# A third of a layer's modulation vectors kept early, two thirds computed one layer later

## The chip, the cores and the metric

The kernel runs on one core of one Trainium2 chip. A core has a matrix engine (TensorE, PE in the rows), a vector engine (VectorE, DVE), a scalar engine with table functions (ScalarE, ACT), a general engine (GpSimd, POOL) and SyncE (SP), which only issues transfers here. ACT and POOL issue transfers too. The metric is the device time of one execution in microseconds (us); the kernel before and the changed one are compared by the median of their timed runs.

## The reference

The program is two layers over 512 latent and 256 context rows of width 1024. What matters here, for each layer l:

```
mod      = silu([c, c_ctx]) @ w_ada[l] + b_ada[l]      # two rows of 6 x 1024
sh1, sc1, ga1, sh2, sc2, ga2 = split(mod, 6)
h        = rmsnorm(x, g_mix[l]) * (1 + sc1) + sh1
parts    = split(h @ w_in[l])                          # 1024 x 2560
y        = [neighbourhood attention, RG-LRU scan, differential attention](parts)
x        = x + ga1 * (y @ w_out[l])
h2       = rmsnorm(x, g_ffn[l]) * (1 + sc2) + sh2
x        = x + ga2 * mixture_of_experts(h2)            # 32 experts, 2 of 8 in one of 4 groups
```

The modulation vectors of a layer depend on c, c_ctx and w_ada[l] alone, not on x. The first third (sh1, sc1) is needed before that layer's projections. The other two thirds (ga1, sh2, then sc2, ga2) are needed only behind its w_out product. w_ada[l] is 24 MB of weights for two rows.

## The kernel before, in words

A layer opens with the norm of x, then forms h as a high and a low half (hh, hl) and runs its input projections. The projections go in chunks of 256 columns of w_in, named by their first column: 768 and 1024 (RG-LRU input), 0, 256, 512 (queries, keys, values of the neighbourhood attention), 2304, 1792, 2048 (values, queries, keys of the differential attention), 1280 and 1536 (gate). A chunk is one 1 MB transfer on SP's queue (line 392); ACT casts it to its high half (line 434) and DVE subtracts for the low half (line 435). A product is 24 matmuls at line 491: high by high, high by low, low by high. A product of context rows or values has 256 columns, one of latent rows 512.

The products stand in a list, `fill`, and `run_fill` (lines 525 to 536) works through it twice in a layer: the first list runs beside the RG-LRU scan, the second beside the neighbourhood attention. Behind every product it fetches the next chunk and calls `step()`. The scan runs in parts (m = 0 to 3, two directions d): for each, gate matmuls on PE (line 753) need an input cast by ACT (xh) and subtracted by DVE (xl, line 435), ACT takes two sigmoids (tt, ii, line 754) and further functions (lines 755, 756, 769), and DVE multiplies and scans (lines 758 and 775 to 793).

`step()` is one modulation step. `ada_steps` (lines 353 to 382) makes a layer's vectors in three groups of 2048 columns, eight steps each. A step is one 1 MB transfer of w_ada on SP's queue (line 360) and four matmuls (line 362) with 32 stationary columns (scp, of which two are real) into the four quarters of one accumulator, acc; the trace records each of the four as two passes. Before a group's first step two small transfers on ACT's queue fetch its bias into adab (line 357). Behind its eighth step DVE adds bias and accumulator into adas (line 367) and ACT's queue carries the two stores to DRAM (line 370); group 0 alone is also transposed and put in columns (lines 374 to 379). Before the change `step()` works only in layer 0. Of the 48 steps eight run at the very start (layer 0, group 0) and 40 stand between layer 0's products: 16 for its own groups 1 and 2, 24 for layer 1.

All w_ada and w_in transfers, and the halves of the chunks, take turns in one ring of six 1 MB buffers (`wtile`, pool `wt`): a transfer waits until the buffer it takes over has been read. An engine works through its instructions in the order of the program, and a scheduler that builds the program has set that order; pools hold the temporary buffers. Later in a layer the same ring carries w_out, and the experts' weights stream through it and through others behind it, by SP.

Of the kernel before, what the change touches and what calls it, by code (L numbers as in the profile page):

```python
# [8 lines left out]
F32 = mybir.dt.float32  # L9
# [3 lines left out]
AF = mybir.ActivationFunctionType  # L13
# [237 lines left out]
def program(tc, a, out, dbg=None):  # L251
# [23 lines left out]
    V, S, G, T = [Chained(e_) for e_ in (nc.vector, nc.scalar, nc.gpsimd, nc.tensor)]  # L275
# [33 lines left out]
    def pacc():  # L309
        return ps.tile([128, 512], F32, name="acc", bufs=1)  # L310
# [24 lines left out]
    cc = con.tile([128, 16], F32, name="cc")  # L335
# [4 lines left out]
    adab = [None, None, None]  # L340
# [9 lines left out]
        else:  # L350
            eng.tensor_copy(o, i)  # L351

    def ada_steps(l):
        for g in range(3):
            acc = pacc()
            for v in range(2):
                S.dma_start(adab[0][v:128:32], a["b_ada"][l].rearrange("(g j f) -> g j f", g=3, j=4)[g])
# [25 lines left out]
    adag = [None, None]  # L383
# [38 lines left out]
    cur = [0]  # L422

    def step(n=1):
        if cur[0] == 0:
            for _ in range(n):
                for g in adag:
                    if next(g, 0) != 0:
                        break

    ct = lambda c_, x_, y_: x_ if c_ else y_

# [19 lines left out]
    for l in range(2):  # L452
# [11 lines left out]
        yp, vp, hp_, xrp, xnp = nxt  # L464
# [3 lines left out]
        if l == 0:  # L468
            trf = hp_.tile([128, 128], F32, name="trf")
            S.dma_start(trf, a["cst"][:, C_TRI:C_MSK])  # L470
            V.tensor_copy(tri, trf)
            scp = hp_.tile([128, 8, 32], F32, name="scp")
            V.memset(scp, 0.0)
            S.activation(scp[:, :, 0:2], cc.rearrange("p (k v) -> p k v", v=2), AF.Silu)
            adab[:] = [hp_.tile([128, 512], F32, name="adab"), hp_, scp]
            G.memset(adab[0], 0.0)
            adag[0] = ada_steps(0)
            adag[1] = ada_steps(1)
        chunks = {}

        def getw(c0):
# [48 lines left out]
        def run_fill(each, then=()):  # L530
            for i_, (c0, f) in enumerate(fill):
                each(i_)
                f()
                for c1 in ([c_ for c_, _ in fill] + list(then))[i_ + 1:i_ + 1 + AHEAD]:
                    getw(c1)
                step()
# [23 lines left out]
        groups = ((4, 2), (0, 2), (2, 2))  # L560
# [948 lines left out]
        def place(s):  # L1509
            return s if s < nm else nm + (s - nm) // 2 if s < nr else s - np_  # L1510

        def column(s):
            return idn[:, place(s), :]
# [459 lines left out]
        for n_ in range(NE + 1):  # L1973
            f = None
            if n_ < NE:
# [4 lines left out]
                else:  # L1980
                    g = Group(column(s), slots[:, place(s):place(s) + 1] if SCT[l] and n_ < NE - 2 else None)
# [104 lines left out]
        g = es[-1].g  # L2086
# [76 lines left out]
```

## Time and profile before

| | |
|---|---|
| timed, median of 3 runs | 2044.59 us |
| lowest, highest | 2043.42, 2047.09 us |
| the profiled execution, its own time | 2047.19 us |
| its span (first to last instruction) | 2045.6 us |
| mean granted TensorE clock | 0.909 |
| busy: PE, DVE, ACT, POOL | 1692.9, 901.0, 575.3, 407.1 us |
| bytes moved | 579.20 MB |

The profile is of one execution, whose time is 2.6 us above the median of the timed runs. Busy shares are averages over stages that differ much: in layer 0 the first list runs from about 60 to 210 us and the second to 341 us; the experts of layer 0 follow to about 1090 us; layer 1's first list runs from about 1125 to 1285 us, its second to 1365 us, and its experts' weights stream from about 1420 us to the end. A granted clock of 1.00 is 2.4 GHz, 0.50 is 1.2 GHz.

### The profile page before, as it was taken

What the parts mean: (1) busy time and instruction counts of PE and PEld (TensorE: products, weight loads), DVE (VectorE), ACT (ScalarE), POOL (GpSimd) and SP (SyncE); (2) the same over time, 40 slices, a digit from 0 to 9 for tenths busy, and PEclk for the clock granted to TensorE, in tenths of its full rate; (3) what the DMA queues carried; (4) which work ended last, traced back from release to release, by engine and by line L of the source; (5) the groups of instructions that cost most, each with busy time, mean ns of one, the idle gap of its engine ahead of it and who ended that gap; (6) DMA issues with size and microseconds to landing.
All of it is one profiled execution on the core that took longest, in us unless ns stands there. A gap on an engine that the chain in (4) does not pass through costs nothing. (4 is left out here: it accounts for less than half of the span.)

```text
span 2045.6 us, 24880 instructions
## 1 busy us (share of the span) xinstructions
PE 1692.9 (83%) x9306; PEld 975.2 (48%) x9306; DVE 901.0 (44%) x1506; ACT 575.3 (28%) x1033; POOL 407.1 (20%) x394
## 2 busy tenths in 40 slices
PE   4998998899697888889895987887959988879773
PEld 3766666676333333333333977566733333333221
DVE  3876443785622212212227698548662122121225
ACT  3563343662111101111113475346411010010011
POOL 1344000443311011001003145104321110010001
PEclk8999999898698998999896989898969989999886
DMA  8537967606799989989986113346469999999994
GB/s 299 203 131 285 322 225 185 165 37 252 275 409 348 407 344 368 417 325 410 401 342 261 58 51 103 125 111 207 188 228 400 404 414 409 410 413 416 416 392 167
DMA packets 153709, 579.20 MB, mean 283 GB/s; under 512 B 18734, under 2 KB 54958, under 8 KB 114672
## 3 DMA queue, kind: packets, MB, share of 16 engines
q1 hardware_dynamic: 142240, 553.35, 71.5%
q0 software_dynamic: 9328, 20.87, 2.9%
q10 hardware_dynamic: 2016, 3.34, 0.5%
q8 instruction: 75, 1.23, 0.2%
q14 instruction: 50, 0.41, 0.1%
HBM read 544.74 MB, written 42.05 MB: 287 GB/s over the span
## 5 line engine op out<-in xcount | busy, mean ns | idle before, releaser
L491 PE MATMUL mm<-hh,w 128*128 128x256 f32 (+1 forms) x960 | 191.5, 343 | 6.6 <-ACT w L434 4.7
L1643 PE MATMUL pss<-w,xT 128*64 128x512 f32 x368 | 170.7, 611 | 7.3 <-DMA w<-in_w_dram 7.3
L1642 PE MATMUL pss<-w,xT 128*64 128x512 f32 x368 | 175.3, 619 | 0.0
L1638 PE MATMUL pss<-w,xT 128*32 128x512 f32 x880 | 140.4, 686 | 37.2 <-DMA w<-in_w_dram 37.2
L491 PEld LDWEIGHTS mm<-hh,w 128*128 128x128 f32 x960 | 150.1, 193 | 37.7 <-issue 9.8
L1826 POOL DMA_INDIRECT xg<-h2d,idx_t x64 | 61.4, 959 | 515.7 <-PE mm L1628 476.8
L1648 PE MATMUL pss<-w,xT 128*128 128x512 f32 x352 | 156.0, 597 | 0.0
L1658 ACT COPY hs<-pss 128x512 f32<-128x512 f32 x53 | 30.9, 582 | 375.6 <-PE pss L1638 221.9
L1517 POOL DMA_INDIRECT yd<-yl,slots x47 | 44.3, 942 | 383.1 <-DVE yl L1562 204.3
L1700 PE MATMUL pss<-w,hT 128*64 128x512 f32 x184 | 102.0, 698 | 9.2 <-DVE hT L1678 8.9
L1648 PEld LDWEIGHTS pss<-w,xT 128*128 128x128 f32 x352 | 65.3, 190 | 89.1 <-issue 83.3
L1678 DVE TENSOR_TENSOR hT<-hT,mm 128x128 f32<-128x128 f32 (+1 forms) x53 | 18.3, 345 | 196.0 <-ACT hT L1677 195.9
L1701 PE MATMUL pss<-w,hT 128*64 128x512 f32 x184 | 102.0, 698 | 0.0
L1558 DVE SCALAR_TENSOR_TENSOR yl<-g,wsl,yl 64x1024 f32<-64x1024 f32 (+2 forms) x32 | 40.8, 1276 | 129.9 <-ACT yl L1553 129.6
L1638 PEld LDWEIGHTS pss<-w,xT 128*32 128x32 f32 x880 | 32.0, 122 | 137.7 <-issue 74.5
L1553 ACT ACTIVATE yl<-g,wsl 64x1024 f32<-64x1024 f32 (+2 forms) x32 | 36.6, 1147 | 211.2 <-DMA yd<-yl,slots 178.6
L1706 PE MATMUL pss<-w,hT 128*128 128x512 f32 x176 | 91.0, 664 | 3.1 <-issue 3.1
L491 PE MATMUL mm<-hl,w 128*128 128x256 f32 (+1 forms) x480 | 93.2, 336 | 0.1
L1562 DVE TENSOR_TENSOR yl<-pss,yl 64x512 f32<-64x512 f32 (+1 forms) x44 | 29.6, 687 | 138.7 <-PE pss L1701 76.0
L351 DVE COPY xT<-mm 128x512 f32<-128x512 f32 (+1 forms) x64 | 36.2, 566 | 101.2 <-PE mm L1628 100.5
L491 PEld LDWEIGHTS mm<-hl,w 128*128 128x128 f32 x480 | 75.4, 190 | 11.1 <-issue 0.8
L1643 PEld LDWEIGHTS pss<-w,xT 128*64 128x64 f32 x368 | 48.8, 140 | 60.3 <-issue 48.2
(377 smaller groups left out, 3263.4 us busy)
## 6 DMA issues: line engine op xcount, KB each, us to landing
w<-in_w_dram SPq DMA_DIRECT2D x382, 1024.0 KB
w<-in_w_ada_dram SPq DMA_DIRECT2D x48, 1024.0 KB
w<-in_w_in_dram SPq DMA_DIRECT2D x20, 1024.0 KB
yd<-bm SPq DMA_DIRECT2D x20, 512.0 KB
w<-yd SPq DMA_DIRECT2D x10, 1024.0 KB
ks<-st SPq DMA_DIRECT2D x16, 384.0 KB
w<-in_w_out_dram SPq DMA_DIRECT2D x5, 1024.0 KB
h2d<-hp SPq DMA_DIRECT2D x10, 512.0 KB
```

The source lines that it names most:

```text
L491: i_ = T.matmul(o, x_(k), y_(k), start=(n == 0), stop=(n == 23))
L1517: G.indirect_dma_start(out=yd[l][0:2 * nrow, :], out_offset=bass.IndirectOffsetOnAxis(ap=idxt, axis=0), in_=rows, in_offset=None, bounds_c ...
L1553: S.activation(self.u[r], g2[r, 1], AF.Copy, scale=b_)
L1558: (V if eng[1] == "V" else G).scalar_tensor_tensor(self.u[r], g2[r, 0], a_, self.u[r], op0=ALU.mult, op1=ALU.add)
L1638: T.matmul(ph[32 * g:32 * g + 32, 0:512], xT[:, k + g // 2, 0:32], w(k + g // 2), start=(k == 0), stop=(k == 6))
L1642: T.matmul(ph[0:64, 0:512], xT[:, k, 0:64], w1(k), start=(k == 0), stop=(k == 7))
L1643: T.matmul(ph[64:128, 0:512], xT[:, k, 0:64], w3(k), start=(k == 0), stop=(k == 7))
L1648: T.matmul(ph[:, o:o + 512], xT[:, k, :], w(k), start=(k == 0), stop=(k == 7))
L1700: T.matmul(py[0:64, :], hT[:, k, 0:64], w2(k, 0), start=(k == 0), stop=(k == 3))
L1701: T.matmul(py[64:128, :], hT[:, k, 0:64], w2(k, 1), start=(k == 0), stop=(k == 3))
L1706: T.matmul(self.p[:, 512 * hf:512 * hf + 512], hT[:, k, :], w2(k, hf), start=(k == 0), stop=(k == 3))
L1826: G.indirect_dma_start(out=o[0:n_, :], out_offset=None, in_=h2d[l][0:nrow, :], in_offset=bass.IndirectOffsetOnAxis(ap=idxt, axis=0), bound ...
```

## The change

`ada_steps` takes a list of groups. Layer 0 now makes only group 0 of layer 1's vectors; layer 1 sets up the stationary tile scp and the bias tile adab anew and makes groups 1 and 2 itself. `step()` works in both layers. So layer 0's lists carry 24 steps in place of 40, and layer 1's first list carries 16.

```diff
--- before.py
+++ after.py
@@ -350,8 +350,8 @@
         else:
             eng.tensor_copy(o, i)
 
-    def ada_steps(l):
-        for g in range(3):
+    def ada_steps(l, groups=(0, 1, 2)):
+        for g in groups:
             acc = pacc()
             for v in range(2):
                 S.dma_start(adab[0][v:128:32], a["b_ada"][l].rearrange("(g j f) -> g j f", g=3, j=4)[g])
@@ -422,11 +422,10 @@
     cur = [0]
 
     def step(n=1):
-        if cur[0] == 0:
-            for _ in range(n):
-                for g in adag:
-                    if next(g, 0) != 0:
-                        break
+        for _ in range(n):
+            for g in adag:
+                if next(g, 0) != 0:
+                    break
 
     ct = lambda c_, x_, y_: x_ if c_ else y_
 
@@ -475,7 +474,14 @@
             adab[:] = [hp_.tile([128, 512], F32, name="adab"), hp_, scp]
             G.memset(adab[0], 0.0)
             adag[0] = ada_steps(0)
-            adag[1] = ada_steps(1)
+            adag[1] = ada_steps(1, (0,))
+        else:
+            scp = hp_.tile([128, 8, 32], F32, name="scp")
+            V.memset(scp, 0.0)
+            S.activation(scp[:, :, 0:2], cc.rearrange("p (k v) -> p k v", v=2), AF.Silu)
+            adab[:] = [hp_.tile([128, 512], F32, name="adab"), hp_, scp]
+            G.memset(adab[0], 0.0)
+            adag[:] = [ada_steps(1, (1, 2))]
         chunks = {}
 
         def getw(c0):
```

In the order of instructions, on PE, near the end of layer 0's second list (hh, hl and w are a product's halves, qa, ka, pe, pT and po belong to the neighbourhood attention). Before:

```order
L491 MATMUL mm<-hh,w 128x256 x8
L491 MATMUL mm<-hl,w 128x256 x8
L491 MATMUL mm<-hh,w 128x256 x8
L362 MATMUL acc<-w,scp 32x512 x4
L899 MATMUL mm<-cst,pe 128x128 x4
L916 MATMUL po<-pT,vv 64x128 x4
L491 MATMUL mm<-hh,w 128x512 x8
L491 MATMUL mm<-hl,w 128x512 x8
L491 MATMUL mm<-hh,w 128x512 x8
L362 MATMUL acc<-w,scp 32x512 x4
L916 MATMUL po<-pT,vv 64x128 x4
```

In the changed kernel, the same place:

```order
L497 MATMUL mm<-hh,w 128x256 x8
L497 MATMUL mm<-hl,w 128x256 x8
L497 MATMUL mm<-hh,w 128x256 x8
L905 MATMUL mm<-cst,pe 128x128 x4
L922 MATMUL po<-pT,vv 64x128 x4
L497 MATMUL mm<-hh,w 128x512 x8
L497 MATMUL mm<-hl,w 128x512 x8
L497 MATMUL mm<-hh,w 128x512 x8
L922 MATMUL po<-pT,vv 64x128 x4
L497 MATMUL mm<-hh,w 128x256 x8
```

The step (the rows with acc) is gone from between the products; all that stands around it keeps its order. Sixteen such groups of four are gone from PE's order between the first list's last value products and the end of the second list.

On PE in layer 1's first list, from a key product (hh,w and hl,w, chunk 256) to the value products behind it (w,hh and w,hl, chunk 512; xh, xl, gh and gl are the operands of the gate matmuls). Before:

```order
L491 MATMUL mm<-hh,w 128x256 x8
L491 MATMUL mm<-hl,w 128x256 x8
L491 MATMUL mm<-hh,w 128x256 x8
L491 MATMUL mm<-w,hh 128x256 x16
L491 MATMUL mm<-w,hl 128x256 x8
L491 MATMUL mm<-w,hh 128x256 x16
L491 MATMUL mm<-w,hl 128x256 x8
L753 MATMUL mm<-xh,gh 128x512
L753 MATMUL mm<-xl,gh 128x512
L753 MATMUL mm<-xh,gl 128x512
L753 MATMUL mm<-xh,gh 128x256
L753 MATMUL mm<-xl,gh 128x256
```

In the changed kernel:

```order
L497 MATMUL mm<-hh,w 128x256 x8
L497 MATMUL mm<-hl,w 128x256 x8
L497 MATMUL mm<-hh,w 128x256 x8
L362 MATMUL acc<-w,scp 32x512 x4
L497 MATMUL mm<-w,hh 128x256 x16
L497 MATMUL mm<-w,hl 128x256 x8
L362 MATMUL acc<-w,scp 32x512 x4
L497 MATMUL mm<-w,hh 128x256 x16
L497 MATMUL mm<-w,hl 128x256 x8
L362 MATMUL acc<-w,scp 32x512 x4
L759 MATMUL mm<-xh,gh 128x512
L759 MATMUL mm<-xl,gh 128x512
```

A step now stands behind each of the first 16 products of the list, three of them in these rows, and the gate matmuls, whose result ACT takes up, stand behind the third.

On ACT in layer 1, at part m = 2 of the scan (v is a store of values, vv their copy). Before:

```order
L754 ACTIVATE tt<-mm,hbr 128x512
L754 ACTIVATE tt<-mm,hbr 128x256
L754 ACTIVATE ii<-mm,hbi 128x512
L754 ACTIVATE ii<-mm,hbi 128x256
L755 ACTIVATE ae<-tt,cfm 128x768
L821 DMA v_8074<-vv 64x256
L756 ACTIVATE tt<-tt,cf 128x768
L754 ACTIVATE tt<-mm,hbr 128x512
L822 DMA v_8074<-vv 64x256
L754 ACTIVATE tt<-mm,hbr 128x256
```

In the changed kernel:

```order
L760 ACTIVATE tt<-mm,hbr 128x512
L370 DMA ada_58<-adas 4x512 x2
L760 ACTIVATE tt<-mm,hbr 128x256
L760 ACTIVATE ii<-mm,hbi 128x512
L760 ACTIVATE ii<-mm,hbi 128x256
L761 ACTIVATE ae<-tt,cfm 128x768
L828 DMA v_7969<-vv 64x256
L762 ACTIVATE tt<-tt,cf 128x768
L357 DMA adab<-in_b_ada_dram 4x512 x2
L760 ACTIVATE tt<-mm,hbr 128x512
L760 ACTIVATE tt<-mm,hbr 128x256
L760 ACTIVATE ii<-mm,hbi 128x512
```

Group 1's two stores of adas stand between the halves of the first sigmoid of one direction, and group 2's two bias transfers ahead of the next direction's first sigmoid.

On ACT at the start of layer 1's second list (raw and rh belong to the RG-LRU state and rotary code, w is a chunk). Before:

```order
L918 COPY yT<-po 128x128
L434 CAST rh<-raw 128x512
L933 COPY raw<-mm 128x512
L434 CAST w<-w 128x2048
L434 CAST rh<-raw 128x512
```

In the changed kernel:

```order
L349 COPY pT<-mm 128x512
L433 CAST rh<-raw 128x512
L433 CAST w<-w 128x2048
L939 COPY raw<-mm 128x512
L924 COPY yT<-po 128x128
```

In both kernels the last cast of a chunk in the first list is the one ahead of this place. Of the casts here the one before is chunk 1280's and follows the copy raw; in the changed kernel it is chunk 2048's, which was cast in the first list before, and it stands between the cast rh and the copy raw.

## Rows read from the trace of the kernel before

**Rows 1.** The page: PE's busy time, share, instructions; the chain that ended last.
```profile
PE 1692.9 (83%) x9306; PEld 975.2 (48%) x9306; DVE 901.0 (44%) x1506; ACT 575.3 (28%) x1033; POOL 407.1 (20%) x394
...
DMA 13%; PE 7%; DVE 1%; ACT 0%; issue 0%; POOL 0%; POOLq 0%; SPq 0%; DVEq 0%; ACTq 0%
```

**Rows 2.** Stages of layer 0: PE, PEld, DVE, ACT, POOL busy (x), clock, DMA share, GB/s.
```profile
208.40:341.20 132.80, 132.12 (x892) 93.00 (x892) 58.26 (x131) 55.48 (x107) 5.85 (x5) 1.00 0.71 242
341.20:360.00 18.80, 10.42 (x41) 7.65 (x40) 8.10 (x12) 4.99 (x9) 3.03 (x2) 0.92 1.05 224
```

**Rows 3.** Line 362 in all: ns min/median/max, first, last; us and times it waited.
```profile
L362 PE MATMUL acc<-w,scp x384: 592/592/617, 23.6 to 332.0; 128*32 128x512 f32 x192
...
  DMA w<-in_w_ada_dram: 11.0, 8
```

**Rows 4.** PE in layer 0: start, us, line, operation, tiles, count, [idle before <-releaser].
```profile
318.96 1.07 PE L362 MATMUL acc<-w,scp 128*32 128x512 f32 x8
319.96 0.66 PE L899 MATMUL mm<-cst,pe 128*128 128x128 f32 x4
```

**Rows 5.** PE behind layer 0's second list, columns as in rows 4.
```profile
342.18 0.74 PE L1132 MATMUL pss<-w,yh 128*128 128x512 f32 x2 [0.93 <-ACT yh L434]
...
357.53 1.62 PE L267 MATMUL pss<-ks,qs 128*128 128x512 f32 x4 [4.94 <-DMA X<-in_x_dram]
```

**Rows 6.** Stages of layer 1's lists, columns as in rows 2.
```profile
1188.50:1285.00 96.50, 68.96 (x441) 62.65 (x441) 87.35 (x78) 55.48 (x74) 44.61 (x26) 0.88 0.29 95
1300.00:1365.00 65.00, 65.00 (x412) 50.16 (x412) 33.63 (x71) 28.98 (x56) 5.08 (x4) 0.98 0.25 82
```

**Rows 7.** PE in layer 1's lists, where it stood idle, columns as in rows 4.
```profile
1193.09 0.57 PE L753 MATMUL mm<-xl,gh 128*128 128x512 f32 x1 [4.56 <-DVE xl L435]
...
1218.77 0.79 PE L753 MATMUL mm<-xl,gh 128*128 128x512 f32 x1 [5.52 <-DVE xl L435]
...
1248.47 0.80 PE L753 MATMUL mm<-xh,gh 128*128 128x512 f32 x1 [7.82 <-ACT tt L754]
...
1284.72 2.08 PE L935 MATMUL mm<-raw,cst 128*128 128x512 f32 x2 [9.51 <-ACT raw L933]
...
1298.75 1.67 PE L935 MATMUL mm<-raw,cst 128*128 128x512 f32 x2 [2.23 <-ACT raw L933]
...
1309.86 1.13 PE L935 MATMUL mm<-raw,cst 128*128 128x512 f32 x2
```

**Rows 8.** ACT in layer 1's first and second lists, columns as in rows 4.
```profile
1220.03 1.11 ACT L754 ACTIVATE tt<-mm,hbr 128x512 f32<-128x512 f32 x2 [2.56 <-PE mm L753]
...
1228.25 0.69 ACT L754 ACTIVATE tt<-mm,hbr 128x512 f32<-128x512 f32 x1 [3.21 <-PE mm L753]
...
1235.20 1.58 ACT L769 ACTIVATE sq<-tt 128x768 f32<-128x768 f32 x2
...
1298.59 1.90 ACT L434 CAST w<-w 128x2048 fp32r<-128x2048 f32 x1
```

**Rows 9.** DVE in layer 1's first list, columns as in rows 4.
```profile
1224.78 1.31 DVE L788 TENSOR_TENSOR_SCAN sq<-tt,ii 128x256 f32<-128x256 f32 x1
...
1236.16 5.15 DVE L775 SCALAR_TENSOR_TENSOR tt<-tt,ae 128x768 f32<-128x768 f32 x2 [0.82 <-ACT sq L769]
...
1279.77 2.27 DVE L435 TENSOR_TENSOR w<-w 128x2048 fp32r<-128x2048 f32 x1
```

**Rows 10.** ACT in layer 0's first list, at a store of adas, columns as in rows 4.
```profile
113.98 1.06 ACTq L370 DMA_DIRECT2D ada<-adas  x2
115.14 1.06 ACT L754 ACTIVATE tt<-mm,hbr 128x512 f32<-128x512 f32 x2 [3.83 <-issue]
```

**Rows 11.** The set-up of scp: engine, line, operation, count, ns, start.
```profile
L473 DVE MEMSET scp<- x1: 272/272/272, 1.2 to 1.2; 128x256 f32 x1
L474 ACT ACTIVATE scp<-cc x1: 217/217/217, 5.9 to 5.9; 128x16 f32<-128x16 f32 x1
```

**Rows 12.** The add of bias and accumulator, columns as in rows 11.
```profile
L367 DVE TENSOR_TENSOR adas<-acc,adab x6: 676/692/693, 33.4 to 332.7; 128x512 f32<-128x512 f32 x6
```

## The prediction

> **What bounds the kernel now.** I read the page first. PE is busy 83% of the span, and the chain that ended last is transfers of expert weights and PE [rows 1], so the change can only tell where it touches PE's own time or a chain that PE waits for. Next I read the time by stretches. In layer 0, from 208.4 to 341.2 us, PE is busy 132.12 of 132.80 us at a granted clock of 1.00, DVE 58.26 and ACT 55.48 [rows 2]: a stage bounded by PE alone. All sixteen steps that leave layer 0 stand in it or within a few us of it. In layer 1 the picture is the reverse. From 1188.5 to 1285 PE is busy 68.96 of 96.50 us and DVE 87.35 [rows 6]: here the chain of the RG-LRU parts through DVE and ACT is the bound, and PE stands idle four times, 4.56, 5.52, 7.82 and 9.51 us, once more 2.23 [rows 7]. From 1300 to 1365 PE is full again [rows 6]. So the work moves from a stretch where PE is the bound to one where it is not, and the question is what the second stretch charges.
>
> **What leaves layer 0.** A step costs PE 1.00 us, start to start: 318.96 to 319.96 [rows 4]. Others of the sixteen read 0.99 to 1.00, so I take sixteen times 0.99, 15.9 us. The steps wait for weights eight times in all, 11.0 us [rows 3], and none of these waits is among the sixteen, since PE loses only 0.68 us in the whole stretch [rows 2]. So 15.9 us is work and nothing else. What is late once it is gone? DVE and ACT have more than half of the stretch free, and the transfers fall by 16 MB from a share of 0.71. Between a score and the transposes that wait for its softmax stand a product and a step; without the step ACT and DVE have 1 us less. I allow 0.5 us (0 to 2) of new waits in all.
>
> Does the gain reach the end? Behind the list PE waits 0.93 us for ACT and later 4.94 us for a transfer of X, in a stretch where the transfer share is 1.05 [rows 2, 5]. If this transfer had a fixed date, up to that whole wait would be lost, and the gain would shrink by what the date does not move. Its buffers and the loads queued ahead of it come free only as PE finishes the list, so I let it move with PE. The experts behind stream by buffers which their predecessors give back, so they move too.
>
> **What layer 1 pays, at its opening.** DVE zeroes scp (0.27 us) and ACT fills two columns (0.22) [rows 11]; POOL clears adab beside other work. The norms of layer 1 hold DVE there: 0.3 us.
>
> **What it pays on PE.** Sixteen steps again, 15.9 us. By the new order four stand ahead of the idle time of 4.56 us (4 times 0.99 is 3.96), four ahead of 5.52 (3.96), three ahead of 7.82 (2.97) and five ahead of 9.51 (4.95): each set is smaller than its gap [rows 7]. They are hidden by waiting for DVE's xl, ACT's tt and ACT's raw. The first two and the ninth also stand ahead of gate matmuls that ACT takes up without such a gap; of these the ninth is covered by ACT's hold below, and one by a cast of ACT that left its place. I count 0.5 us. If DVE or ACT were not late, PE would show the full 15.9.
>
> **What it pays on ACT.** Group 1's two stores wait in ACT's queue for DVE's add. In layer 0 the trace has the same case: the stores start at 113.98 and the sigmoid behind them at 115.14, after 3.83 us of idle time in which its matmuls were long done [rows 10]. In layer 1 the sigmoid ahead of the stores starts at 1220.03 [rows 8]; it comes some 2 us later, since more convolution pieces now stand ahead of xl on DVE. The add follows the scan that starts at 1224.78 and takes 1.31 us [rows 9]. With the same 2 us, less what those pieces no longer cost behind xl, it ends near 1227.9 (0.69 us [rows 12]), and the stores are out near 1229. The second half, two ii, ae and the next function (about 4 us) carry ACT to 1233, where the next direction's sigmoid starts, 5 us behind its 1228.25 [rows 8]. From there the path runs through ACT's sq at 1235.20 and DVE's products at 1236.16, which waited for sq [rows 8, 9], so DVE is 5 us late. The bounds: nothing, if the add comes before ACT is ready, and 7 if ACT stands from 1222 to 1229 and none of it is made up. I take 5, which lies by the 3.83 of layer 0 plus the transfer of the delay by xl.
>
> The Trainium skill's "TensorE: Matmul & The Clock Gate", in its table of specifications, says that ScalarE's queue is strictly first in, first out, and this speaks against the change: by it the hold costs everything behind the stores, as the 3.83 us show. Could a waiting store be passed by, the hold would be 0 and the sum 5 us lower.
>
> **What it pays on DVE and at the seam.** The splits of the chunks slide by one: 2304's takes the place that 1792's had, 1792's that of 2048's at 1279.77 (2.27 us [rows 9]), and 2048's falls into the second list. In the first list that is one split fewer at the front and none fewer at the end, so I count nothing. Group 2's add stands at the end of DVE's chain: 0.7 us [rows 12]. In the second list chunk 2048's cast now stands between ACT's rh and its copy raw, for which PE waited 2.23 us [rows 7]. It takes 1.90 [rows 8], and I count 1.5 (0 to 1.9). Chunk 2048's own transfer, behind the last step and eight stores on SP, can start about when this list ends, some 10 us ahead of its cast; I count nothing for it.
>
> **The sum.** Minus 15.9 in layer 0, plus 0.5 there; plus 0.3, 0.5, 5, 0.7 and 1.5 in layer 1: minus 7.4 us. From the profiled execution's 2047.2 that is 2039.8. That execution lies 2.6 us above the median of the timed runs, so against the median of 2044.6 I forecast 2037. By the bounds of the terms, layer 1 pays 0.5 to 12 and layer 0 gives back 0 to 2 of its 15.9, so this case runs from 2029 to 2043.
>
> **The rivals.**
>
> All hidden: ACT's hold is made up by idle time of DVE, and layer 1 pays about 1 us. The sum is then minus 15, 2029.5. For it: every set of steps fits its gap, and DVE still has about 9 us of idle time. Against it: the 3.83 us in layer 0 [rows 10]. A further gain belongs here. Behind a gap PE runs slower: the two matmuls of raw take 2.08 us at 1284.72 and 1.67 at 1298.75 against 1.13 later [rows 7]. With steps in the gap that could fall away, 1 to 3 us at the head of the second list: 2027. The Trainium skill's page on the clock gate says under its heading on oscillation that idle gaps bring the lower clock and cost the matmuls behind them; by it the steps would pay for themselves there, and rows 7 agree as far as the slow matmuls behind each gap go.
>
> Work only moved: layer 0's gain meets a date that does not move. If the transfer behind the list [rows 5] is late by itself, 4.94 us of the gain is gone, and with the 8 of layer 1 minus 2.5 is left, 2042; with a hold of 7 and no cover for the cast it is zero, 2044.6.
>
> Slower: the steps do not fall into the gaps but in front of them. PE takes its instructions in order, and each set of steps stands ahead of gate matmuls for which ACT waits already (2.56 and 3.21 us, [rows 8]). If a delay of the chain at one part shifts the next part's gap, PE's 15.9 us and ACT's hold are paid one after the other: 15.9 plus 5, 0.7, 0.3 and 1.5 is 23.4, against 15.4 gained. That is plus 8, 2052.5. It decides from where layer 1 pays more than 15.4 us. Against it: DVE, not PE, ended three of the gaps, directly or through ACT.
>
> **How the numbers follow.** The forecast has 0.50, all hidden 0.23, work only moved 0.15, slower 0.12. A measurement of this kernel can tell about 0.2%, 4.1 us, from no change. Of the forecast's case 0.40 is faster than that by more; with 0.23 of all hidden and 0.05 of the moved case this makes 0.68 faster. Slower by over 0.2% is most of the last rival and a little of the third: 0.12. The rest, 0.20, is no change that can be told. The range leaves out the lowest tenth and the last rival's upper part: 2027 to 2047.
>
> **What would show it.** In layer 0 no line 362 between 209 and the end of the second list, and that list's last product about 15 us sooner, with all that follows up to layer 1's opening moved by the same. In layer 1 rows of line 362 in the places of the idle times, those shorter by about 4, 4, 3 and 5 us; on ACT a gap of 5 us or more ahead of the second half of a sigmoid near the first store of adas; the first matmul of raw about 5 to 6 us later within its layer. Wrong it would be if PE's stretches in layer 0 gained new waits as long as the steps, if the layer's opening did not come sooner, or if layer 1's two lists grew by more than 12 us.

## The result, and the profile after

The changed kernel takes 2020.28 us (median of 6 runs, 2015.89 to 2029.39) beside 2047.52 us for the kernel before on the same chip (6 runs): a ratio of 0.9878, 95% interval 0.9853 to 0.9903. A second series (e9 below) gave 0.9866, 0.9838 to 0.9894. It is 25 to 27 us faster where the sum of the forecast was 7.4: the direction was right, and the time lies below the range. In the code of the changed kernel lines behind the first are shifted by up to 6: line 941 is 935 of before, 497 is 491, 760 is 754, 1089 is 1083.

The page of the profiled execution, as in [rows 1]: PE's row, and the chain that ended last.

```profile
PE 1688.6 (84%) x9306; PEld 977.0 (48%) x9306; DVE 902.0 (45%) x1507; ACT 575.4 (29%) x1034; POOL 405.3 (20%) x395
...
DMA 13%; PE 7%; DVE 1%; ACT 0%; issue 0%; POOL 0%; POOLq 0%; SPq 0%; DVEq 0%; ACTq 0%
```

The same number of matmuls, the same chain, and a span of 2014.7 us. Nothing in these rows says where the time went, so I cut both traces at the same events of PE. Each cell is the time from the event ahead of it, in us; "range" is over executions of the same program in that stretch.

| stretch | before, two traces | changed, two traces | mean difference |
|---|---|---|---|
| layer 0: last transposes of adas to first w_out matmul | 133.8, 134.9 | 115.2, 115.2 | -19.2 |
| w_out to first score | 15.3, 15.1 | 13.0, 13.2 | -2.1 |
| to layer 0's routing | 172.7, 171.9 | 172.5, 171.6 | -0.2 |
| layer 0's experts | 579.6, 580.5 | 573.9, 589.5 | (range 574 to 590) |
| layer 1: opening to first gate matmul | 60.1, 61.1 | 62.3, 62.8 | +2.0 |
| to first raw cast product | 114.8, 114.9 | 119.0, 118.6 | +4.0 |
| to last raw cast product | 41.6, 42.2 | 35.8, 37.8 | -5.1 |
| to w_out | 40.2, 40.2 | 40.2, 40.2 | 0 |
| w_out to first score | 17.2, 16.8 | 11.7, 11.8 | -5.3 |
| to the end | 661.8, 663.1 | 662.7, 661.0 | -0.6 |

From the start to the first of these events all four take 207.6 to 208.4 us. Without the experts of layer 0 the differences add to -26.5, and the two ratios make 25 and 27 us. The experts' stretch scatters by 16 us in one and the same changed kernel, so the 573.9 of the first profile (4 us under its median) is no effect of the change. The stretch to layer 0's routing scatters too, though not in these four: with layer 0 as in the changed kernel it took 163.2 us in e8 and 167.2 in e12. The 1.1 us between the two traces of before in the first row are one step's wait for its weights, 1.07 us, that only the second has.

The first of the stages of layer 0 in [rows 2]:

```profile
208.40:322.60 114.20, 113.53 (x764) 90.26 (x764) 57.01 (x129) 54.90 (x107) 5.88 (x5) 1.00 0.43 144
```

PE stands idle 0.67 us in it, as before (0.68), and has lost 128 matmul records, sixteen steps; its busy time falls by 18.59. Line 362 in all, and what it waited for, as in [rows 3]:

```profile
L362 PE MATMUL acc<-w,scp x384: 592/593/1062, 20.0 to 1246.1; 128*32 128x512 f32 x192
...
  DMA w<-in_w_ada_dram: 15.9, 11
```

This sum, like the 11.0 us and eight times of [rows 3], counts the weight loads (PEld) along with the matmuls; PE's own rows have five waits of 6.2 us in all, and four of 4.0 before. All stand ahead of 208 us in layer 0; none of the steps waits for weights in layer 1. PE behind layer 0's second list, as in [rows 5]:

```profile
323.51 0.73 PE L1138 MATMUL pss<-w,yh 128*128 128x512 f32 x2 [0.87 <-ACT yh L433]
...
336.55 0.94 PE L267 MATMUL pss<-ks,qs 128*128 128x512 f32 x4 [1.10 <-DMA X<-in_x_dram]
```

The wait for X has shrunk from 4.94 to 1.10. Layer 1's first list, from the same event to within 0.3 us of the first product of raw, as in [rows 6], and PE's waits in it and behind it, as in [rows 7]:

```profile
1163.90:1264.20 100.30, 85.16 (x563) 65.66 (x562) 87.22 (x78) 55.19 (x74) 39.80 (x26) 0.92 0.55 197
```

```profile
1195.50 0.80 PE L759 MATMUL mm<-xl,gh 128*128 128x512 f32 x1 [4.83 <-DVE xl L434]
...
1226.69 0.80 PE L759 MATMUL mm<-xh,gh 128*128 128x512 f32 x1 [6.98 <-ACT tt L760]
...
1260.36 3.29 PE L497 MATMUL mm<-hh,w 128*128 128x512 f32 x8 [2.79 <-DVE w L434]
...
1264.32 1.14 PE L941 MATMUL mm<-raw,cst 128*128 128x512 f32 x2 [0.68 <-ACT raw L939]
...
1274.08 1.12 PE L941 MATMUL mm<-raw,cst 128*128 128x512 f32 x2
```

PE is busy 16.20 us longer in a window 3.80 us longer: most of the steps fill idle time. The wait of 4.56 us is gone, those of 5.52 and 7.82 are smaller by 0.7 and 0.8 only, though four and three steps stand ahead of them, the 9.51 has become 2.79 and 0.68, and the 2.23 ahead of the second product of raw is gone. ACT at group 1's stores, as in [rows 8], and the add that they wait for, as in [rows 12]:

```profile
1199.68 0.69 ACT L760 ACTIVATE tt<-mm,hbr 128x512 f32<-128x512 f32 x1
1201.83 1.11 ACTq L370 DMA_DIRECT2D ada<-adas  x2
1202.98 0.47 ACT L760 ACTIVATE tt<-mm,hbr 128x256 f32<-128x256 f32 x1 [2.61 <-DVE sq L796]
```

```profile
1201.13 0.66 DVE L367 TENSOR_TENSOR adas<-acc,adab 128x512 f32<-128x512 f32 x1
```

This is the predicted hold, at its place: the add ends at 1201.79, the stores go out at 1201.83, and the second half of the sigmoid comes 2.61 us late though its matmuls were done. (The row names DVE's sq, which ends in the same moment; that it was the stores shows in e4, where they are gone from this place and the gap with them.)

### The profile page after: what moved, and what is told of

It is laid out like the page before. It is cut to its first block, busy times and chain, and to the rows that moved or that the text cites. A ratio compares the mean times of both kernels' runs of the same rounds, so it can differ in the third digit from the quotient of the medians.

```text
span 2014.7 us, 24883 instructions
## 1 busy us (share of the span) xinstructions
PE 1688.6 (84%) x9306; PEld 977.0 (48%) x9306; DVE 902.0 (45%) x1507; ACT 575.4 (29%) x1034; POOL 405.3 (20%) x395
## 5 line engine op out<-in xcount | busy, mean ns | idle before, releaser
L1649 PE MATMUL pss<-w,xT 128*64 128x512 f32 x368 | 173.4, 619 | 7.0 <-DMA w<-in_w_dram 7.0
L1648 PE MATMUL pss<-w,xT 128*64 128x512 f32 x368 | 177.7, 626 | 0.0
```

The source lines that it names most:

```text
L1648: T.matmul(ph[0:64, 0:512], xT[:, k, 0:64], w1(k), start=(k == 0), stop=(k == 7))
L1649: T.matmul(ph[64:128, 0:512], xT[:, k, 0:64], w3(k), start=(k == 0), stop=(k == 7))
```

## The experiments

Where a kernel is timed, its ratio is to the kernel before on the same chip. The stretches named are those of the table.

**e1: the memory alone.** The kernel before, with three dead tiles of the sizes of scp, adab and adas (5 KB a partition) in layer 1, and no step moved.

```diff
+        else:
+            for n_, w_ in (("scp", 256), ("adab", 512), ("adas", 512)):
+                G.memset(hp_.tile([128, w_], F32, name=n_), 0.0)
```

> The kernel before, with one addition: in layer 1's h pool three tiles of the sizes of scp, adab and adas (5 KB a partition together) are made and cleared once by POOL. No step moves. Theory A (the moved memory frees the tail's transfers): the first transfer behind layer 1's second list, gfc, no longer waits for the list's last product, PE's wait for X<-xd falls from 9.5 to about 2.5 us, and the time falls by 5 to 8 us; layer 0 is as before, with its 4.9 us wait for X. Theory B (the part of the gain beyond the steps is how far single executions lie apart, the layout does nothing): no change, and the wait for X<-xd stays near 9.5.

2044.4 us, ratio 0.9986 (0.9967 to 1.0005). The median doesn't resolve it, but the stretch from w_out to the first score does: 12.0 us instead of 17.2, with nothing changed but where tiles lie and three clears on POOL. What happens is seen on SP's queue, in its order (start, us, line, operation). Before, layer 0 and then layer 1 (gfc is the scale of the second norm):

```profile
333.40 0.34 SPq L1083 DMA_DIRECT2D gfc<-in_g_ffn_dram  x1
...
345.86 3.09 SPq L1065 DMA_DIRECT2D X<-in_x_dram  x4
...
1363.61 0.33 SPq L1083 DMA_DIRECT2D gfc<-in_g_ffn_dram  x1
...
1372.35 3.75 SPq L1065 DMA_DIRECT2D X<-xd  x4
```

In the changed kernel:

```profile
281.38 1.48 SPq L1089 DMA_DIRECT2D gfc<-in_g_ffn_dram  x1
...
327.26 2.53 SPq L1071 DMA_DIRECT2D X<-in_x_dram  x4
...
1310.49 1.61 SPq L1089 DMA_DIRECT2D gfc<-in_g_ffn_dram  x1
...
1343.17 2.79 SPq L1071 DMA_DIRECT2D X<-xd  x4
```

And in e1:

```profile
1339.94 1.70 SPq L1086 DMA_DIRECT2D gfc<-in_g_ffn_dram  x1
...
1372.34 2.70 SPq L1068 DMA_DIRECT2D X<-xd  x4
```

A small transfer, gfc, stands at the head of this part of SP's queue. Before, in layer 1, it started 2.9 us ahead of w_out (1366.53), and all behind it on the queue was late. What it waited for is read from times, as no trace shows addresses: PE's last pass over h's low half, in the last product of the second list, ends at 1363.58, 0.03 us ahead of it:

```profile
1361.56 2.02 PE L491 MATMUL mm<-hl,w 128*128 128x512 f32 x8
```

In e8, below, the two times are 1342.19 and 1342.21. So I take its tile to lie in what was hl's memory. With 5 KB more in that pool it no longer waits for this pass and starts 30 us ahead of w_out. In layer 0 of before it starts at 333.40, 0.03 us behind the end of the last add into adas (332.7 [rows 12]); in the changed kernel no add stands that late. The first score of layer 1, in before and in the changed kernel and e1:

```profile
1383.77 1.62 PE L267 MATMUL pss<-ks,qs 128*128 128x512 f32 x4 [9.54 <-DMA X<-xd]
```

```profile
1351.96 0.94 PE L267 MATMUL pss<-ks,qs 128*128 128x512 f32 x4 [2.43 <-DMA X<-xd]
```

```profile
1381.40 1.32 PE L267 MATMUL pss<-ks,qs 128*128 128x512 f32 x4 [2.70 <-DMA ks<-st]
```

**e2: layer 0's half alone.** The sixteen steps are left out altogether, and layer 1 reads layer 0's vectors in place of its own groups 1 and 2.

```diff
-            adag[1] = ada_steps(1)
+            adag[1] = ada_steps(1, (0,))
...
-            Y.dma_start(vc[:, v], ada_d[l][v, 3072:5120].rearrange("(c p k) -> p c k", c=2, k=8))
+            Y.dma_start(vc[:, v], ada_d[0][v, 3072:5120].rearrange("(c p k) -> p c k", c=2, k=8))
```

> The kernel before without groups 1 and 2 of layer 1's vectors: their 16 steps are left out altogether, and layer 1 reads layer 0's vectors in their place. Layer 1's memory is as before. It measures what layer 0 gives back. Theory A: layer 0's second list ends 18.7 us sooner (16 times 1.17, a step with the drain at its two edges), the wait for X in layer 0 falls from 4.9 to about 1, layer 1's wait for X<-xd stays at 9.5: 21 us faster, ratio about 0.990. Theory B: 16 to 18.7 us faster and the wait for X in layer 0 only moves: ratio 0.991 to 0.992. My prediction's count (0.99 a step): 15.4 us, ratio 0.9925.

Its time, 2224.19 us, says nothing: with other vectors in layer 1 the stretch behind its first score alone takes 856.9 us in place of 662, which I put down to rows that go to other experts. Up to layer 1's lists the trace can be read: layer 0's stretch is 115.2 us and w_out to score 12.9, as in the changed kernel (gfc starts at 280.12 here), so these two gains are layer 0's own. From the opening of layer 1 to the gate it takes 60.1 and on to the first raw 114.9, the numbers of before: what the changed kernel has more there, the steps and their tiles bring. The tiles alone bring none of it: in e1 these stretches are 60.1 and 112.8.

**e3: the steps in layer 1's second list.** As the change, but step() keeps its test of cur[0], and this line ahead of layer 1's second list lets it work there.

```diff
+        cur[0] = 0
```

> The changed kernel, but layer 1's 16 steps stand in its second list (and behind it) and not in its first. Theory A (in the first list the steps are hidden by the scan's waits, in the second PE is the bound): layer 1's two lists together take 16 times 1.17, 18.7 us, more than in the changed kernel, less some 3 us for the hold of ACT that is gone from the first list; the tail's transfers wait for the last add again, some 5 us: about 20 us above the changed kernel, within 6 us of the kernel before. Theory C (a step beside the scan costs PE as much as beside products): the same time as the changed kernel.

2051.32 us, ratio 1.0027 (1.0009 to 1.0045). The first list costs 115.0 as before, and from the first raw product to w_out 106.6 us pass instead of 81.8 before and 76.0 in the changed kernel. That is 24.8 to 30.6 us for the steps where 18.7 was expected, and 30 us above the changed kernel where 20 was. Against before, PE is busy 18.0 us longer there: it has no idle time to give. The rest is waits: the steps behind the list wait 3.5 us for weights, and w_out waits 5.37 for ACT in place of 1.09. So the place decides, not the removal from layer 0.

**e4: stores and biases off ACT's queue.** The changed kernel, with layer 1's transfers of lines 357 and 370 issued by GpSimd.

```diff
...
-                S.dma_start(dst, sb[v:128:32, :])
+                (G if l == 1 and g else S).dma_start(dst, sb[v:128:32, :])
```

> The changed kernel, with layer 1's stores of adas and its bias transfers issued by POOL and not by ACT. It measures ACT's hold. Theory A: ACT's 2.6 us of idle time at the store is gone, DVE's products behind it start about 4 us sooner in the layer, and the first matmul of raw too; the second list's head loses part of this: 1 to 4 us faster than the changed kernel, ratio to the kernel before 0.986. Rival: POOL's own work for the scan stands behind the waiting stores and is late by as much: no change against the changed kernel (0.988) or 1 to 3 us slower.

2017.44 us, ratio 0.9859 (0.9835 to 0.9883). The two halves of the sigmoid stand side by side again on ACT:

```profile
1202.49 1.05 ACT L760 ACTIVATE tt<-mm,hbr 128x512 f32<-128x512 f32 x2
```

So the hold is real: the gap of 2.61 us was the stores'. By the Trainium skill's "TensorE: Matmul & The Clock Gate" (table of specifications) ScalarE's queue is strictly first in, first out; the trace agrees, with 2.61 us behind the stores and none without them.

From gate to raw it takes 116.9 us instead of 119.0, but these 2.1 us are not what the hold cost, and DVE's products do not start 4 us sooner, as the theory had it. DVE's last product of this kind, in before, in the changed kernel and in e4:

```profile
1266.80 0.94 DVE L775 SCALAR_TENSOR_TENSOR tt<-tt,ae 128x768 f32<-128x768 f32 x1
```

```profile
1244.66 0.93 DVE L781 SCALAR_TENSOR_TENSOR tt<-tt,ae 128x768 f32<-128x768 f32 x1
```

```profile
1248.63 0.94 DVE L781 SCALAR_TENSOR_TENSOR tt<-tt,ae 128x768 f32<-128x768 f32 x1
```

Counted from the layer's first gate matmul (1169.90, 1145.28, 1147.83) this is 96.9, 99.4 and 100.8 us. So the steps delay the scan's chain by 2.5 us, and taking the hold away gives none of it back (in e4 DVE stands 2.54 us for one of PE's value products ahead of this row, at 1238.30). The 2.1 us arise behind this row. The last stores wait in POOL's queue for DVE's add, and POOL's work on bm (the bias and mask of the neighbourhood attention) stands behind them. In the changed kernel bm runs beside DVE's last scan, in e4 behind it:

```profile
1248.07 8.48 POOL L866 TENSOR_TENSOR bm<-b,b 128x1024 f32<-128x1024 f32 x3 [0.30 <-DMA b<-in_cst_dram]
...
1251.13 3.21 DVE L796 TENSOR_TENSOR_SCAN sq<-tt,sq,ii 128x512 f32<-128x512 f32 x1
```

```profile
1253.12 1.28 DVE L796 TENSOR_TENSOR_SCAN sq<-tt,sq,ii 128x512 f32<-128x512 f32 x1
...
1257.63 8.15 POOL L866 TENSOR_TENSOR bm<-b,b 128x1024 f32<-128x1024 f32 x3
```

The scan takes 1.28 us instead of 3.21, and the rows ahead of it and behind it 0.69 and 1.17 instead of 2.68 and 3.21. In the 14 traces this scan takes 3.2 us where bm starts ahead of the first of the three rows (eight traces) and 1.28 where it starts behind it (six). That moves the first raw product with no step moved at all: in e1 and e11, where bm starts 1.3 to 1.4 us later since it waits for its own transfer, gate to raw takes 112.8 us where before has 114.8.

**e5: five steps late.** The changed kernel, with the last five of layer 1's steps in the second list.

```diff
-                step()
+                if not last or i_ < 11 or then == ():
+                    step()
```

> The changed kernel with the last five of layer 1's 16 steps behind the first five products of its second list, so that PE stands idle again ahead of the first matmul of raw. Theory A (part of the second list's head gains because PE no longer stood idle: the slow matmuls behind the gap are gone): the gap of some 9 us and the slow rows come back (two matmuls of raw 2.1 us in place of 1.14, eight of scores 2.1 in place of 1.13), about 2 us, and the five steps cost 5 times 1.17, 5.9 us, in the second list where PE is the bound; the first list loses nothing or up to 1 us less. From the gate matmuls to layer 1's w_out 7 to 9 us more than in the changed kernel; ratio to before 0.9915. Rival (the head gains by the new order of ACT's copies alone): the matmuls of raw stay at 1.14 us behind the gap, and 4 to 6 us are lost.

2034.11 us, ratio 0.9925 (0.99 to 0.9949). The stretch from gate to raw falls to 111.2, and of the 9.51 ahead of the first raw product only 1.76 comes back, without slow rows (the product takes 1.13); but from first to last raw it takes 51.8 against 35.8, with a new wait:

```profile
1276.68 2.25 PE L906 MATMUL mm<-cst,pe 128*128 128x128 f32 x8 [5.91 <-DVE pe L899]
```

From gate to w_out this is 204.6 us, 9.6 more than in the changed kernel where 7 to 9 was expected. But the gap whose slow rows it was to bring back did not come, so it doesn't decide between its theory and its rival. The wait of 5.91 is another's: DVE's pe stood 2.39 us for POOL's bm, and bm 8.25 for its transfer.

**e6: group 2 alone moves.** Layer 0 keeps layer 1's groups 0 and 1; eight steps move.

```diff
-            adag[1] = ada_steps(1, (0,))
+            adag[1] = ada_steps(1, (0, 1))
...
-            adag[:] = [ada_steps(1, (1, 2))]
+            adag[:] = [ada_steps(1, (2,))]
```

> Half of the change: layer 0 keeps groups 0 and 1 of layer 1's vectors, and layer 1 makes group 2 alone, 8 steps. Theory A (1.17 us a step in layer 0; the tails' transfers are freed by the memory, whatever the number of steps): layer 0's second list ends 8 times 1.17, 9.3 us, sooner than before; the wait for X in layer 0 is about 1 us and that for X<-xd about 2.5 as in the changed kernel; ratio to before 0.993 to 0.991. With 0.99 a step it would be 7.9 us; if the transfers' gains grow with the steps, half of each.

2037.08 us, ratio 0.9949 (0.9932 to 0.9966). Layer 0 gains 7.5 us of the 18.6, less than half. The trace shows two waits that the first traces of the two kernels don't have in this stretch, 0.48 us of a step for its weights (at 220.48, where e10 has its 1.07) and this:

```profile
281.78 1.13 PE L941 MATMUL mm<-raw,cst 128*128 128x512 f32 x2 [1.44 <-ACT raw L939]
```

With these 1.92 us the eight steps gave 9.4, 1.18 each, as the sixteen (18.6, or 1.16).

**e7: e4 with each step two products later.**

```diff
-                step()
+                if not last or i_ > 1:
+                    step()
```

> The changed kernel with stores and bias transfers on POOL, and with layer 1's steps behind products 3 to 18 of its first list in place of 1 to 16. Theory A: the first two steps stood ahead of gate matmuls without a gap, so from the layer's opening to the first gate matmul 1.2 us come back, and from there to the first matmul of raw another 0 to 2; but two more steps stand at the end of the list, where PE waited 2.8 us for a split: 1 to 3 us faster than the changed kernel with stores on POOL, ratio to before 0.985. Rival (the steps at the end delay the second list): same or 2 us slower than that kernel.

2024.34 us, ratio 0.9885 (0.9866 to 0.9903). From the opening to the gate it takes 60.0 us, as before: the 2.2 there were the first two steps, which stand ahead of the first gate matmuls. But from gate to raw it takes 118.9, 2 us more than e4: the later steps put the last add and its stores behind bm, so that bm runs beside DVE's scan again (3.23 us). And from first to last raw it takes 41.0: the wait of 2.23 us of before ahead of the second raw product is there again. So its ratio lies at its rival's and not below e4's (the two intervals overlap).

**e8: the changed kernel, its three tiles in another pool.**

```diff
-            scp = hp_.tile([128, 8, 32], F32, name="scp")
...
+            scp = rgp.tile([128, 8, 32], F32, name="scp")
...
+            adab[:] = [rgp.tile([128, 512], F32, name="adab"), rgp, scp]
```

> The changed kernel with layer 1's scp, adab and adas in the scan's pool and not in the h pool, so that the second list's tail lies in memory as before. Theory A (the 5 KB in the h pool free the tail's first transfer from the wait for the last product): the stretch from layer 1's first w_out matmul to its first differential score goes from 11.7 back to about 17 us, PE's wait for X<-xd from 2.4 to 8 or 9: 4 to 6 us slower than the changed kernel, ratio to before 0.990. Theory B (the wait for X<-xd differs by single executions): it stays at 2 to 4 us.

2029.21 us, ratio 0.9931 (0.9903 to 0.9958). The same steps in the same list, but gfc is issued 2.9 us ahead of w_out (1342.21 and 1345.13), as before, and the wait is back:

```profile
1342.21 0.33 SPq L1089 DMA_DIRECT2D gfc<-in_g_ffn_dram  x1
```

```profile
1361.48 1.62 PE L267 MATMUL pss<-ks,qs 128*128 128x512 f32 x4 [7.10 <-DMA X<-xd]
```

With e1 this shows the cause both ways. The stretch of raw is 42.7 here, also back at the value of before; that led to e11.

**e9 and e10: both kernels once more**, for their spread.

> The changed kernel once more, for a narrower ratio and a second trace. Theory: the parts outside the experts' stretch of layer 0 come back (first stretch of layer 0 about 115.2 us, opening to first gate product 62.3, gate to first raw product 119.0, first raw to last raw 35.8, w_out to first score of layer 1 about 11.7), which add to 26 us less than before, so a ratio of 0.987 (0.985 to 0.990). Rival: part of the 27 us of the medians is chance of one placement of the runs, and the ratio comes out at 0.990 to 0.996; then the experts' stretch of layer 0, 573.9 us in the first trace, would be 579 to 587 here, and the gain of that stretch was none.

> The kernel before once more, for the spread of one trace. Theory: the experts' stretch of layer 0 (579.6 us in the first trace, 573.9 to 588.8 in the kernels run since, though several of them run the same program there) scatters by several us in one and the same kernel, while the stretches around the change stay within 0.5 us: 133.8 to the first w_out product of layer 0, 60.1 from the opening of layer 1 to the first gate product, 114.8 to the first raw product, 41.6 to the last, 17.2 from w_out to the first score. Rival: the experts' stretch comes back at 579 to 580, so that its differences between kernels are effects of the kernels.

e9: 2022.99 us, ratio 0.9866 (0.9838 to 0.9894), about 27 us again. Its trace has layer 0's experts at 589.5 us against 573.9, and e10's 580.5 against 579.6; e11 and e1, whose layer 0 is that of before, have 582.5 and 586.3. So this stretch scatters by itself. Outside it the stretches around the change came back within 0.5 us in e9 (that of raw is told next), and within 1.1 in e10 where 0.5 was expected. One thing of the first trace did not come back: the first product of raw has the same wait ahead of it in e9, but takes 2.08 us, not 1.14.

```profile
1278.76 2.08 PE L941 MATMUL mm<-raw,cst 128*128 128x512 f32 x2 [0.68 <-ACT raw L939]
```

**e11: the order of two copies alone.** The kernel before, with ACT's first copy yT<-po of layer 1 held behind its copy of the second raw product (ropes["c"] is the copy at line 933).

```diff
-            S.copy(yT[:, j, 128 * i:128 * i + 128], po[:, 0:128])
+            y_ = S.copy(yT[:, j, 128 * i:128 * i + 128], po[:, 0:128])
+            if last and (i, j) == (0, 0):
+                behind(y_, ropes["c"])
```

> Kernel before, with one order pinned: ScalarE's first copy yT<-po of layer 1 stands behind its copy of the second raw product instead of ahead of it, which is how the changed kernel has it. Theory (the order of two ScalarE copies makes TensorE's wait of 2.23 us ahead of the second raw cast product): that wait goes, and the stretch from the first raw product to the last falls from 41.6 us to about 39, by 2.2 to 3; the rest stays, ratio about 0.9985. Rival (the wait goes only because TensorE was not idle ahead of the first raw product, the slow rows of 2.08 us there being the cause): nothing changes, the stretch stays at 41 to 42.6, and the wait of about 2.2 us stands there.

2044.67 us, ratio 0.9993 (0.9975 to 1.0011): too little for the median. In the trace the wait is gone, and with it the slow rows behind it, so that the third product follows 9.53 us behind the second, not 11.11 [rows 7]:

```profile
1284.15 2.08 PE L937 MATMUL mm<-raw,cst 128*128 128x512 f32 x2 [7.59 <-ACT raw L935]
...
1296.90 1.13 PE L937 MATMUL mm<-raw,cst 128*128 128x512 f32 x2
...
1306.43 1.12 PE L937 MATMUL mm<-raw,cst 128*128 128x512 f32 x2
...
1315.29 1.22 PE L899 MATMUL mm<-cst,pe 128*128 128x128 f32 x8 [0.95 <-DVE rc L891]
```

From the first to the third product it takes 22.28 us against 25.14 [rows 7]: the slow rows behind the first product last 0.9 us longer here, or it would be 3.8 less. Then 0.95 comes back as a new wait, and the stretch is 39.9 (41.6 and 42.2 before). The first product is as slow as before, so the rival (its slowness makes the wait) falls. ACT shows why, before:

```profile
1296.57 0.27 ACT L918 COPY yT<-po 128x128 f32<-128x128 f32 x1 [5.00 <-PE po L916]
1296.73 0.62 ACT L434 CAST rh<-raw 128x512 fp32r<-128x512 f32 x1
1298.11 0.59 ACT L933 COPY raw<-mm 128x512 f32<-128x512 f32 x1 [0.76 <-DVE rl L435]
```

The copy yT stands first and waits 5.00 us for PE's po, the last work of PE ahead of the second raw product; only behind it come the cast rh, DVE's rl, and then the copy raw, for which PE waits. The order decides in the other traces too. Where yT stands first and no step stands beside the raw products (before, e10, e1, e2, e6, e7, e8) PE waits 2.22 or 2.23 us for the second raw product; where the copy raw stands first (the changed kernel, e9, e4, e11, e12) it waits 0.29 in e4 and none is shown in the others.

**e12: e4, each step one product later, and the order of e11.**

```diff
-                step()
+                if not last or i_ > 0:
+                    step()
```

> The changed kernel with three edits: stores and biases of layer 1's steps issued by GpSimd, the steps behind products 2 to 17 of the first list instead of 1 to 16, and the order of the two ScalarE copies pinned as the changed kernel has it. Theory (the costs add): opening to first gate product back to about 60.0 us (changed kernel 62.3), gate to first raw about 118 (119.0), first raw to last raw 36 to 38.5 (35.8; 41.0 in the kernel with later steps without the pinned order), so 2 to 3 us less than the changed kernel, ratio to before about 0.9855. Rival (the stretch of the raw products is short only because TensorE comes to it late and busy): what the first list gives back returns there as a wait, the sum is that of the changed kernel, ratio 0.987 to 0.988.

2022.8 us, ratio 0.9892 (0.9864 to 0.992): no better than the changed kernel. The first list gave back what was expected (61.1 and 116.5, 3.8 us less than the changed kernel; 2.5 of it from gate to raw, with bm behind DVE's scan as in e4), but the stretch of raw took 41.2. The wait for the second product is not there; one for the third is, since ACT's copy (at 1277.90) stands behind the cast of a chunk whose transfer came late:

```profile
1278.53 1.75 PE L944 MATMUL mm<-raw,cst 128*128 128x512 f32 x2 [4.40 <-ACT raw L942]
```

```profile
1276.09 1.90 ACT L433 CAST w<-w 128x2048 fp32r<-128x2048 f32 x1 [3.13 <-DMA w<-in_w_in_dram]
```

On SP the transfers of the second list's chunks are issued 0.5 and 14.0 us behind the first raw product, where the changed kernel issues them 2.4 us ahead of it and 8.0 behind. That the steps' place on SP's queue does this was not tried. No version beats the changed kernel by more than the intervals; e4's (0.9835 to 0.9883) overlaps both of its own.

## Why the prediction was wrong

- **What leaves layer 0, -15.9: mis-sized, it is -18.6 by the first trace.** A step was priced by its own rows, start to start 0.99. What it costs is seen only across its neighbours. Before, with a step between two value products, and in the changed kernel without it:

```profile
210.76 1.11 PE L491 MATMUL mm<-w,hl 128*128 128x256 f32 x8
211.80 1.07 PE L362 MATMUL acc<-w,scp 128*32 128x512 f32 x8
212.79 2.17 PE L491 MATMUL mm<-w,hh 128*128 128x256 f32 x16
214.79 1.11 PE L491 MATMUL mm<-w,hl 128*128 128x256 f32 x8
```

```profile
210.70 1.11 PE L497 MATMUL mm<-w,hl 128*128 128x256 f32 x8
211.65 2.06 PE L497 MATMUL mm<-w,hh 128*128 128x256 f32 x16
213.55 1.11 PE L497 MATMUL mm<-w,hl 128*128 128x256 f32 x8
```

  From product to product 4.03 us with the step, 2.85 without: 1.18, of which 0.99 is the step, 0.09 the edge ahead and 0.10 the edge behind. Sixteen times 1.16 is the 18.6, and e6's eight agree. The step's matmuls run on tiles of 128*32, the products' on 128*128, as the rows name them. The Trainium skill's "TensorEngine Tiling (Array Packing)", Key Properties, says that a change of the tiling mode drains TensorE; the trace agrees, with about 0.1 us at either edge. No run changes the tiles alone, so the share of the tiling in these 0.2 us is not shown.
- **New waits in layer 0, +0.5:** none, 0.67 us against 0.68. (That none of the sixteen steps waits for weights held for the first trace; in e10 one waits 1.07.)
- **The tail behind layer 0's list: "I let it move with PE".** It moved further, by 2.1 us, since gfc, the transfer ahead of it on SP, waited for the steps' own adas (without them it starts at 280.12 in e2, not 333.40). The moved-work rival, a transfer with a fixed date, was wrong the other way round.
- **Layer 1's opening and first steps, +0.8: mis-sized, +2.0.** PE has no gap there; two steps of 1.17 are 2.3, and e7 takes them away. The sentence "covered by a cast of ACT that left its place" did not hold.
- **The steps on PE, "hidden", and ACT's hold, +5, with the add, +0.7: the number came out near, the mechanism did not.** The stretch from gate to raw grew by 4.0 us, so with the opening layer 1's first list pays 6.0 where 6.5 was forecast. The hold stands where it was foreseen, with 2.61 us, but no run shows that it costs anything: without it the scan's chain comes no sooner (100.8 us in e4 against 99.4). What the sum had at nothing costs instead. The steps, of which "each set is smaller than its gap", stand ahead of gate matmuls on which the chain hangs; with all or part of them in the first list DVE's last product starts at 99.3 to 101.3 us (eight traces), without them there at 96.9 to 97.0 (before, e10, e1, e2, e3, e11). These 2.5 us are the mechanism of the "slower" rival, at a fraction of its price. The other 1.5 stand behind it, about 0.4 on DVE with the add, and the rest on PE's last product, whose last pass waited 2.79 us for DVE's split and ran 3.29 us, where the same pass takes 2.02 elsewhere. That the sum met the 6 us is luck.
- **The seam, +1.5: the step that failed with the wrong sign, -5.1.** The predicted cast ahead of the copy raw is there, but the copy yT left the same place, which the list of ACT's order ahead of the prediction shows. I priced what came in and not what went out. By e11's rows, in the kernel before, that order alone takes out 2.2 us of wait and 1.6 of slow rows behind it; the slow rows at the first product, another 2.0 us, are gone in only one of the two traces of the changed kernel.
- **The tail behind layer 1's list: not in the sum at all, -5.3.** The wait for X (9.5 us) was not read, and the new tiles were priced by the instructions that fill them, not by the memory they take (e1, e8). With the seam, 6.6 us off, these two make 12 of the 19 us between the forecast's sum and the table's; layer 0 makes 6.

So the forecast's -15.4 in layer 0 was -21, and its +8 in layer 1 was -4.4. "All hidden" was nearest in number, and of the hold its reason (made up by idle time) is what the runs show; but the steps were hidden only in part, and the two tails and the seam, 12.5 us together, it did not have. Its clock gain can be seen at the second raw product, behind a wait that went for another reason, and not reliably at the first. "Slower" needed the steps to stand in front of the gaps: in the first list they cost 2.5 us of the chain that way, and in e3, where PE has no gaps, all of theirs.

## What to carry to other kernels

Price a group of instructions by the distance of its neighbours with and without it, not by its own rows; where tile shapes change, both edges count. Read a change of order on each engine for what leaves a place too, and follow each waiting engine to the instruction at the head of its queue. When an experiment gains in a stretch, follow the chain through the stretch and see at which row the gain arises: e4 was built to take out one wait, took it out, and gained by another. A temporary buffer can cost or give more by whose memory it pushes aside than by the work it brings: look at the first transfer of each queue behind a stage, and ask what last read the memory under it.

## What was not expected of the hardware

One transfer that had to wait for its tile held all transfers behind it on SP's queue: a wait of 9.54 us at the score became 2.43 to 2.70 as that one was issued 30 us ahead of w_out instead of 2.9. A scan on DVE took 3.21 us beside POOL's work on bm and 1.28 without it. And the same two matmuls behind the same wait of 0.68 us took 1.14 us in one execution and 2.08 in another (granted clock 1.00 and 0.81 in the 12 us from there), so that a clock gain at one place is not to be counted from one trace.
